# Part of the modulation weight loads issued by GpSimd instead of SyncE, in a four-layer DiT on one core

## The chip, the core and the metric

The kernel runs on one core of a Trainium2 chip. The core has a matrix engine (TensorE, PE in the profile, with its weight loads shown as PEld), a vector engine (VectorE, DVE), a scalar engine (ScalarE, ACT), a general engine (GpSimd, POOL) and a small engine that here does nothing but issue transfers (SyncE, SP). Each engine works through its own list of instructions in order; semaphores tell one engine that another, or a transfer, is done. The metric is device time in microseconds (us) of one execution, lower is better.

## The reference, cut to what matters

Four layers work on `x` (256 tokens of 2048 channels) and a context `ctx` of the same size, in fp32: layers 0 and 3 mix with a Fourier transform, layer 1 is attention with a window and the context, layer 2 is a conformer convolution. Every layer begins and ends with a modulation, and its weights are what this change is about:

```python
def ada_modulation(cond, w, b):
    m = jax.nn.silu(cond) @ w + b
    return jnp.split(m, 3, axis=-1)
...
    for i in range(DEPTH):
        ...
        shift, scale, gate = ada_modulation(c, ada_w[i], ada_b[i])
        h = rms_norm(x, norm_g[i]) * (1.0 + scale[:, None, :]) + shift[:, None, :]
        shift_c, scale_c, gate_c = ada_modulation(c_ctx, ada_w[i], ada_b[i])
        hc = rms_norm(ctx, norm_g[i]) * (1.0 + scale_c) + shift_c
        ...
        x = x + gate[:, None, :] * o
        if with_ctx:
            ctx = ctx + gate_c * oc
    return rms_norm(x, final_g)
```

`ada_w[i]` is 2048 x 6144 in fp32, 50 MB for each layer. It multiplies only two vectors (`c` and `c_ctx`), so almost all its cost is bringing it in.

## The kernel before, in words

**Matrix products.** Weights are loaded in pieces of 128 x 1024 (`raw`, issued on SP at L153, L155 and L157). ScalarE rounds each piece to a high half (`whi`, L181), and VectorE, in layer 2 partly GpSimd, takes the rest as a low half (`wlo`, L182). PE multiplies three times, high by high, low by high, high by low (L194 to L196 with the weights standing, L214 to L216 with the tokens standing).

**Modulation.** The 12 thirds of modulation weights are numbered (l, s): layer l, and s = 0 for shift, 1 for scale, 2 for gate. Shift and scale of layer 0 are computed by `ada_tiles` (L221) at the start. All others go through two objects of the class `Stream`: `ada_a` has (0,2), (1,0) and (1,1) and multiplies on PE (L271); `ada_v` has (1,2), (2,0), (2,1), (2,2), (3,0), (3,1), (3,2) and accumulates on DVE (L282 for the first piece of a third, L284 for the others), apart from a part of layer 2 in which it, too, uses PE. A third has 16 steps, and each step loads two tiles `aw` of 128 x 1024 (512 KB) in `Stream.get`, L331: 320 loads in all. The tiles come from one ring of four buffers (AWB = 4, tag "aw"), which both streams share, and two tiles of `ada_tiles` as well (L226). So a load can be issued only when the tile four places before it has been used up.

When a third on DVE is complete, its sum `adacc` is folded by PE (L298), copied (L301), transposed by small matmuls (L303), and becomes a part of `modc` (L309, L313). `adacc` has one buffer (L277): the next third cannot begin before that fold.

**Order.** The code calls `pump`, `step` and `until` of the streams between pieces of the matrix products (`plan` sets how many steps fall on how many pieces). That order is only a wish. The framework's scheduler then places every instruction in its engine's list by its own model of when operands and queues become free. An instruction's place in an engine's list can therefore change when a transfer is put on another queue, though no code near it was touched.

**Stages** in the profile of before: the start, with x, ctx and the first tiles of layer 0, until about 70 us; layer 0's z and shift/scale together to about 250 us, the rest of layer 0 to 700; keys and values of layer 1 (`do_kv`, L906) to 830; its attention (`do_q` L882, `do_attn` L939) to 1024; its z product and output product (L1003, L1023) to 1182; then layers 2 and 3.

**What shares SP with the loads.** Besides L331, SP issues all raw weights, the loads of x and ctx (L620), and the tiles of `ada_tiles` (L231). ScalarE issues a few small loads at the start. GpSimd issues none; it fills a few small tiles at the start (L112 and others) and first works again at about 1174 us, with the low halves of layer 2.

Names for the steps below: `cT` is ctx transposed (L642), `hh`/`hl` the halves of layer 0's normalised input (L449, L450), `accz`, `accq`, `acco` the accumulators of the products for z, queries and output, `pT` and `v` the transposed probabilities and the values of attention, `po` its output (L970), `nmx` its row maxima (L958, L959).

Of the kernel before, what the change touches and what calls it, by code (L numbers as in the profile page):

```python
# [19 lines left out]
P = 128  # L20
D = 2048
# [47 lines left out]
def dit_kernel(ctx: ExitStack, tc: tile.TileContext, x, c, ctxt, c_ctx, norm_g, ada_w, ada_b,  # L69
               four_w_in, four_w_out, attn_w_in, attn_sink, attn_w_out, conv_w_in, conv_dw_w,  # L70
               conv_dw_b, conv_ln_g, conv_ln_b, conv_w_out, final_g, dft, rope, maskc, out):
    nc = tc.nc
# [16 lines left out]
    def nm(s):  # L89
        uid[0] += 1  # L90
        return f"{s}_{uid[0]}"
# [226 lines left out]
    class Stream:  # L318
# [7 lines left out]
        def get(self, l, s, kt):  # L326
            aw = []
            for h in range(2):
                t = wp.tile([P, D // 2], F32, tag="aw", bufs=AWB, name=nm("aw"))
                c0 = s * D + h * (D // 2)  # L330
                nc.sync.dma_start(t[:], ada_w[l, kt * P:(kt + 1) * P, c0:c0 + D // 2])  # L331
                aw.append(t)
            return aw

# [668 lines left out]
    for g in range(4):  # L1003
        accs = [accA("accz") for _ in range(2)]
        gemm_T(outs2(accs), lambda kt: w_piece(w_rows(wi, kt, 2560 + g * 512)), rhsx, range(0, KT, 2), pump1)
        for i in range(2):
# [4 lines left out]
            t = hp.tile([P, 2, 512], F32R, tag=f"hc{2 * g + i}", name=nm("yh1"))  # L1011
# [106 lines left out]
    for cg in range(8):  # L1118
# [8 lines left out]
        for ci in range(2):  # L1127
            kt = 2 * cg + ci
# [207 lines left out]
```

## Time and profile before

| | before |
|---|---|
| median of 3 runs | 1928.31 us (1928.18 to 1931.59) |
| profiled execution | 1930.65 us |
| its span, first to last instruction | 1928.5 us |
| instructions in the span | 30124 |
| mean granted PE clock | 0.986 of full speed |
| bytes moved | 433.63 MB, mean 225 GB/s |
| loads `aw` (L231 and L331) | 376 issues of 512 KB on SP, median 5.4 us to landing |

The profile is one execution recorded by the hardware. Times in it are on its own scale: 2.15 us lie outside the span, and this execution was 2.34 us longer than the median. Busy time tells how full an engine is; the chain that ended last tells what released what, followed back from the end. An engine's idle time matters only where PE, or whatever sets the end of a stage, waits for it.

### The profile page before, as it was taken

Reading aid. Unit: us, or ns where it says so; the run is one execution under the profiler, and the core shown is the slowest. Engines: PE = TensorE matmul, PEld = TensorE weight load, DVE = VectorE, ACT = ScalarE, POOL = GpSimd, SP = SyncE. Lnnn points to the kernel's source line nnn. Section 1 sums busy time; section 2 is a strip of 40 time slices with the busy share of each in tenths; the row PEclk is TensorE's granted clock in tenths of the full one; section 3 lists DMA queues with packets and bytes.
Section 4 is the critical chain, followed back from the end, with each engine's and each line's share of the span. In section 5 each row is a group of like instructions: output and inputs, shape, how many; then the busy total and the mean of one; then the engine's idle time right before and its main releaser. Section 6 shows DMA issues by size and latency. Waiting matters only on the chain.

```text
span 1928.5 us, 30124 instructions
## 1 busy us (share of the span) xinstructions
PE 1852.9 (96%) x11143; PEld 1506.8 (78%) x11143; DVE 1441.8 (75%) x2719; ACT 892.7 (46%) x1606; POOL 228.0 (12%) x127
## 2 busy tenths in 40 slices
PE   6999999999999999999999999899998998999997
PEld 5566657777766787766689887899998887899886
DVE  4899944566654459977897796588899998897675
ACT  6333342224331236465555445444445656556553
POOL 0000000000000000000000002788880002000000
PEclk9999999999999999999999999999998998999999
DMA  8888878666677745831667695476765795876553
GB/s 257 282 297 301 300 245 271 206 232 207 233 269 265 272 151 161 275 120 55 206 208 251 227 320 197 159 232 212 234 230 175 245 322 169 290 273 176 163 175 131
DMA packets 247236, 433.63 MB, mean 225 GB/s; under 512 B 16214, under 2 KB 135734, under 8 KB 247090
## 3 DMA queue, kind: packets, MB, share of 16 engines
q1 hardware_dynamic: 245664, 430.00, 67.5%
q10 hardware_dynamic: 1426, 1.73, 0.3%
q8 instruction: 87, 1.43, 0.3%
q14 instruction: 59, 0.48, 0.1%
HBM read 429.56 MB, written 2.10 MB: 224 GB/s over the span
## 4 chain that ended last, share of the span: by engine, by line
PE 78%; DVE 9%; DMA 6%; issue 3%; ACT 2%; POOL 0%; SPq 0%; DVEq 0%; ACTq 0%; POOLq 0%
PE acco L1040 8%; PE accz L194 6%; PE accz L195 6%; PE accz L196 6%; DMA aw<-in_ada_w_dram 5%; PE acco L1041 4%; PE accu L214 4%; PE accu L215 4%; PE accu L216 4%; PE pa L271 3%; PE accg L194 3%; PE accg L196 3%; PE accg L195 3%; PE acco L194 3%; DVE wlo L182 3%
## 5 line engine op out<-in xcount | busy, mean ns | idle before, releaser
L181 ACT CAST whi<-raw 128x512 fp32r<-128x512 f32 (+1 forms) x764 | 540.8, 758 | 693.0 <-PE accz L195 133.0
L182 DVE TENSOR_TENSOR wlo<-raw,whi 128x512 fp32r<-128x512 f32 x680 | 492.0, 770 | 202.4 <-ACT whi L181 197.7
L182 POOL TENSOR_TENSOR wlo<-raw,whi 128x1024 fp32r<-128x1024 f32 x84 | 203.8, 2434 | 1371.6 <-ACT whi L181 1370.6
L284 DVE SCALAR_TENSOR_TENSOR adacc<-aw,csil,adacc 128x1024 f32<-128x1024 f32 x188 | 243.9, 1302 | 85.7 <-DMA aw<-in_ada_w_dram 85.2
L1040 PE MATMUL acco<-yh,whi 128*128 128x512 f32 x768 | 270.4, 397 | 0.2 <-DVE xT L1048 0.2
L196 PE MATMUL accz<-hx,wlo 128*128 128x256 f32 x768 | 221.1, 289 | 12.1 <-DVE wlo L182 12.0
L195 PE MATMUL accz<-hx,whi 128*128 128x256 f32 x768 | 220.9, 288 | 3.6 <-DVE hx L450 3.6
L194 PE MATMUL accz<-hx,whi 128*128 128x256 f32 x768 | 220.9, 288 | 1.1 <-ACT hx L449 1.1
L1041 PE MATMUL acco<-yh,wlo 128*128 128x256 f32 x768 | 215.2, 280 | 1.2 <-DVE wlo L182 1.2
L1139 DVE SCALAR_TENSOR_TENSOR pv<-gp,dwT,pv 128x256 f32<-128x256 f32 x480 | 191.1, 482 | 24.8 <-ACT pv L1133 24.4
L1040 PEld LDWEIGHTS acco<-yh,whi 128*128 128x128 f32 x768 | 144.1, 188 | 34.6 <-ACT yh L479 0.8
L196 PEld LDWEIGHTS accz<-hx,wlo 128*128 128x128 f32 x768 | 150.1, 196 | 14.1 <-DVE wlo L182 13.1
L195 PEld LDWEIGHTS accz<-hx,whi 128*128 128x128 f32 x768 | 150.3, 196 | 5.4 <-DVE hx L450 4.2
L194 PEld LDWEIGHTS accz<-hx,whi 128*128 128x128 f32 x768 | 150.3, 196 | 3.0 <-ACT hx L449 1.8
L196 PE MATMUL accg<-hx,wlo 128*128 128x256 f32 x512 | 146.6, 286 | 2.8 <-POOL wlo L182 2.7
L194 PE MATMUL accg<-hx,whi 128*128 128x256 f32 x512 | 147.5, 289 | 1.1 <-ACT hx L449 1.1
L1041 PEld LDWEIGHTS acco<-yh,wlo 128*128 128x128 f32 x768 | 144.8, 189 | 2.2 <-DVE wlo L182 2.1
L195 PE MATMUL accg<-hx,whi 128*128 128x256 f32 x512 | 146.4, 286 | 0.0
L194 PEld LDWEIGHTS accg<-hx,whi 128*128 128x128 f32 x512 | 99.6, 195 | 8.5 <-issue 6.9
L194 PE MATMUL acco<-yh,whi 128*128 128x512 f32 (+1 forms) x272 | 105.0, 387 | 0.0
L196 PEld LDWEIGHTS accg<-hx,wlo 128*128 128x128 f32 x512 | 99.6, 195 | 4.3 <-POOL wlo L182 3.4
L195 PE MATMUL acco<-yl,whi 128*128 128x512 f32 (+1 forms) x272 | 102.8, 378 | 0.0
(261 smaller groups left out, 3579.9 us busy)
## 6 DMA issues: line engine op xcount, KB each, us to landing
aw<-in_ada_w_dram SPq DMA_DIRECT2D x376, 512.0 KB, 5.4
raw<-in_four_w_in_dram SPq DMA_DIRECT2D x126, 512.0 KB, 4.6
raw<-in_attn_w_in_dram SPq DMA_DIRECT2D x72, 512.0 KB, 3.6
raw<-in_conv_w_in_dram SPq DMA_DIRECT2D x128, 256.0 KB, 2.9
raw<-in_four_w_out_dram SPq DMA_DIRECT2D x32, 512.0 KB, 6.7
raw<-in_attn_w_out_dram SPq DMA_DIRECT2D x64, 256.0 KB, 4.3
raw<-in_conv_w_in_dram SPq DMA_DIRECT2D x32, 512.0 KB, 4.4
raw<-in_conv_w_out_dram SPq DMA_DIRECT2D x64, 256.0 KB, 4.6
```

Of the source, the lines that this page charges most:

```text
L181: nc.scalar.copy(hv[:, c], iv[:, c])
L182: eng.tensor_sub(lv[:, c], iv[:, c], hv[:, c].bitcast(F32))
L194: mm(o, a, hh, start=st, stop=False, skip_group_check=True)
L195: mm(o, a, hl, start=False, stop=False, skip_group_check=True)
L196: mm(o, b, hh, start=False, stop=kt + k == span[1] - 1, skip_group_check=True)
L214: mm(acc[:], hh, whi[:, k, :], start=st, stop=False)
L215: mm(acc[:], hh, wlo[:, k, :], start=False, stop=False)
L216: mm(acc[:], hl, whi[:, k, :], start=False, stop=kt + k == KT - 1)
L284: ins = nc.vector.scalar_tensor_tensor(acc[:, cs], aw[i][:], cc, acc[:, cs], op0=ALU.mult, op1=ALU.add)
L1040: mm(o[:], whi[:, k, cs], rhs(kt), start=kt == 0, stop=False, skip_group_check=True)
L1041: mm(o[:, :256], wlo[:, k, cs], rhs(kt)[:, :256], start=False, stop=kt == KT - 1, skip_group_check=True)
L1139: nc.vector.scalar_tensor_tensor(pv[:, :256], gt[:, t:t + 256], dwT[:, kt, t:t + 1], pv[:, :256], op0=ALU.mult, op1=ALU.add)
```

## The change

One line: which engine issues the load in `Stream.get`.

```diff
             for h in range(2):
                 t = wp.tile([P, D // 2], F32, tag="aw", bufs=AWB, name=nm("aw"))
                 c0 = s * D + h * (D // 2)
-                nc.sync.dma_start(t[:], ada_w[l, kt * P:(kt + 1) * P, c0:c0 + D // 2])
+                (nc.sync if l == 3 or s == 2 and l == 2 else nc.gpsimd).dma_start(t[:], ada_w[l, kt * P:(kt + 1) * P, c0:c0 + D // 2])
                 aw.append(t)
             return aw
```

GpSimd now issues the six thirds (0,2), (1,0), (1,1), (1,2), (2,0) and (2,1): 6 x 16 x 2 = 192 loads. SP keeps (2,2) and layer 3, 128 loads. The condition covers layer 0's gate as well. Bytes, tiles and buffers are the same. SP's list becomes 192 rows shorter and GpSimd's 192 longer, and the scheduler's order changes on the other engines.

The first place is the start. GpSimd's list begins, after its small fills, with loads of the third (1,2):

```order
L112 MEMSET one_78 128x1
L331 DMA aw_2097<-in_ada_w_dram 128x1024
L331 DMA aw_2099<-in_ada_w_dram 128x1024
L331 DMA aw_2104<-in_ada_w_dram 128x1024
L331 DMA aw_2106<-in_ada_w_dram 128x1024
L331 DMA aw_2110<-in_ada_w_dram 128x1024
L331 DMA aw_2112<-in_ada_w_dram 128x1024
```

aw_2104 and aw_2106 take the buffers that `ada_tiles` used and wait for PE's last use of them; each later load waits for the accumulate four places before. In SP's list of before, aw_2097 stood behind the loads of L231.

DVE's list at that place, before, where transposed ctx (cT) is copied out:

```order
L450 SCALAR_TENSOR_TENSOR hl_325<-tmp_365,modc_87,hh_324 128x256
L182 TENSOR_TENSOR wlo_303<-raw_300,whi_302 128x2x128x2
L642 COPY cT_116<-pxt_449 128x512
L642 COPY cT_118<-pxt_463 128x512
L642 COPY cT_120<-pxt_477 128x512
L648 TENSOR_REDUCE ssc<-ssn 128x2
```

and now, with accumulates into adacc_2101, the sum of (1,2):

```order
L450 SCALAR_TENSOR_TENSOR hl_325<-tmp_365,modc_87,hh_324 128x256
L182 TENSOR_TENSOR wlo_303<-raw_300,whi_302 128x2x128x2
L284 SCALAR_TENSOR_TENSOR adacc_2101<-aw_2104,csil,adacc_2101 128x1024
L284 SCALAR_TENSOR_TENSOR adacc_2101<-aw_2106,csil,adacc_2101 128x1024
L284 SCALAR_TENSOR_TENSOR adacc_2101<-aw_2110,csil,adacc_2101 128x1024
L284 SCALAR_TENSOR_TENSOR adacc_2101<-aw_2112,csil,adacc_2101 128x1024
L284 SCALAR_TENSOR_TENSOR adacc_2101<-aw_2116,csil,adacc_2101 128x1024
L642 COPY cT_116<-pxt_449 128x512
L284 SCALAR_TENSOR_TENSOR adacc_2101<-aw_2118,csil,adacc_2101 128x1024
L642 COPY cT_118<-pxt_463 128x512
L642 COPY cT_120<-pxt_477 128x512
L648 TENSOR_REDUCE ssc<-ssn 128x2
```

Six accumulates have moved up among the copies. Further ones follow: aw_2130, aw_2134, aw_2136 and aw_2140 stand ahead of the low half wlo_667, where none of them stood before. By place in the list, aw_2097 goes from row 49 to 29, aw_2110 from 123 to 41, aw_2140 from 201 to 69.

The second place is the end of layer 1, after attention: DVE's list around the first accumulates of (2,2) (adacc_9165, loads on SP in both). Before, they stood inside attention:

```order
L990 TENSOR_TENSOR on_7522<-po_7582,rb_7607 128x256
L182 TENSOR_TENSOR wlo_8231<-raw_8228,whi_8230 128x512
L282 TENSOR_SCALAR adacc_9165<-aw_9161,csil 128x1024
L958 TENSOR_REDUCE nmx_7836<-s_7841 128x1
L282 TENSOR_SCALAR adacc_9165<-aw_9163,csil 128x1024
L959 TENSOR_TENSOR nmx_7836<-nmx_7836,nsink 128x1
L958 TENSOR_REDUCE nmx_7838<-s_7855 128x1
L284 SCALAR_TENSOR_TENSOR adacc_9165<-aw_9264,csil,adacc_9165 128x1024
```

Now they stand among the low halves of z's weights, with the fold's last steps (modc_89) between them:

```order
L182 TENSOR_TENSOR wlo_9171<-raw_9168,whi_9170 128x512 x2
L282 TENSOR_SCALAR adacc_9165<-aw_9161,csil 128x1024
L182 TENSOR_TENSOR wlo_9203<-raw_9200,whi_9202 128x512 x2
L309 TENSOR_TENSOR modc_89<-pa_9148,adabT 128x16
L282 TENSOR_SCALAR adacc_9165<-aw_9163,csil 128x1024
L313 SCALAR_TENSOR_TENSOR modc_89<-modc_89,ngT 128x16
L284 SCALAR_TENSOR_TENSOR adacc_9165<-aw_9264,csil,adacc_9165 128x1024
L182 TENSOR_TENSOR wlo_9235<-raw_9232,whi_9234 128x512 x2
```

The start of (2,2) went from row 1001 to row 1183 of DVE's list. On PE, the fold of (2,1) that frees adacc (L298, pa_9148) was split in one matmul at row 3326, among `accq`, and three at row 3686, just ahead of a `po` of attention; it is now at rows 3944 and 4310, among the `accz` matmuls of z, the last of them behind attention's last `po` (row 4183). From attention's end to layer 2, DVE's list now holds all 32 accumulates of (2,2) and the first 18 of (3,0), where 23 accumulates lay before.

In the stage of keys and values, three accumulates (aw_8360, aw_8362 and aw_8860) now stand ahead of rope (L850, L856) and of the low halves wlo_7039 and wlo_7059.

## The prediction

> **What bounds the kernel now.** I read the shares of busy time first, then the chain that ended last, then a table of busy time by stage.
>
> ```profile
> PE 1852.9 (96%) x11143; PEld 1506.8 (78%) x11143; DVE 1441.8 (75%) x2719; ACT 892.7 (46%) x1606; POOL 228.0 (12%) x127
> ...
> PE 78%; DVE 9%; DMA 6%; issue 3%; ACT 2%; POOL 0%; SPq 0%; DVEq 0%; ACTq 0%; POOLq 0%
> ```
>
> TensorE is busy for 96% of the span, and 78% of the chain lies on it. The chain also runs 9% over VectorE (DVE) and 6% over transfers, so I looked at such an excursion before believing in it. Around 600 us the chain leaves PE and comes back:
>
> ```profile
> 584.03 4.03 DMA aw<-in_ada_w_dram
> 588.09 1.29 DVE adacc L284
> ...
> 601.85 8.18 DMA aw<-in_ada_w_dram
> 610.07 1.03 PE pa L271 x4
> ```
>
> The excursion covers 26 us, but PE worked through it; the PE timeline shows what the wait at its end was worth, 0.72 us:
>
> ```profile
> 610.07 1.03 PE L271 MATMUL pa<-aw,csil 128*2 128x512 f32 x4 [0.72 <-DMA aw<-in_ada_w_dram]
> ```
>
> So a modulation load on the chain is not yet time to be won. By stage (columns: window, length, busy PE, PEld, DVE, ACT, POOL, clock, DMA share, GB/s):
>
> ```profile
> 5.00:30.00 25.00, 15.99 (x89) 10.73 (x90) 12.36 (x33) 15.48 (x35) 0.00 (x0) 0.93 1.08 327
> 30.00:40.00 10.00, 9.23 (x84) 7.61 (x82) 3.27 (x7) 9.75 (x25) 0.00 (x0) 1.00 0.31 90
> 40.00:70.00 30.00, 27.78 (x167) 17.23 (x165) 19.86 (x38) 12.66 (x21) 0.00 (x0) 1.00 0.91 299
> 70.00:250.00 180.00, 175.99 (x849) 118.89 (x850) 166.95 (x250) 73.46 (x91) 0.00 (x0) 1.00 0.83 285
> 250.00:700.00 450.00, 447.86 (x2230) 327.32 (x2230) 238.28 (x405) 135.48 (x252) 0.00 (x0) 1.00 0.73 247
> 700.00:830.00 130.00, 124.56 (x617) 100.42 (x615) 108.81 (x213) 62.75 (x140) 0.00 (x0) 1.00 0.61 197
> 830.00:1024.00 194.00, 194.00 (x1222) 141.39 (x1221) 163.84 (x410) 118.68 (x285) 0.00 (x0) 1.00 0.46 144
> 1024.00:1182.00 158.00, 156.54 (x1061) 141.54 (x1061) 118.28 (x189) 75.75 (x136) 4.58 (x2) 1.00 0.79 259
> ```
>
> From 250 to 1182 us PE idles 2.1 + 5.4 + 0.0 + 1.5 = 9.0 us of 932. That is the most that any better feeding can win there. What can be lost has no such bound: DVE stands at 93% in 70 to 250 us and at 75% in 1024 to 1182, and the transfers at 299 to 327 GB/s in three stages.
>
> **What leaves SP.** 192 of the 320 loads of L331 change queue.
>
> ```profile
> L331 SPq DMA_DIRECT2D aw<-in_ada_w_dram x320: 327/341/1258, 38.3 to 1720.0; - x160
> ...
> DMA to landing us min/median/max: 3.6/5.5/8.3
> ```
>
> SP is relieved of 192 x 0.341 = 65 us of issue work and of a part of its waits for buffers:
>
> ```profile
> SPq L331 <- DVE adacc L284: 101.8, 87, 5.2
> ...
> SPq L331 <- PE pa L271: 101.2, 40, 5.6
> ...
> SPq L331 <- DMA aw<-in_ada_w_dram: 83.8, 30, 5.8
> ```
>
> Those 286.8 us held the weight loads behind them, but PE's 9.0 us of idle time say that the weights were there anyhow. Loads that SP now brings sooner are worth what PE still waited for. Of that, only its waits for modulation rows are directly the change's own:
>
> ```profile
> PE pa L271 <- DMA aw<-in_ada_w_dram: 1.6, 4, 0.7
> ```
>
> I take **-1.6 us**, with 0 and half of 9.0 (-4.5) as ends.
>
> **The start.** The trace of before has no load on GpSimd's queue. The nearest rows are the same loads on SP: 5.5 us over the whole run, and in the first 60 us
>
> ```profile
> aw<-in_ada_w_dram SPq DMA_DIRECT2D x10, 512.0 KB, 6.3
> ```
>
> with 8.3 us the longest of all. GpSimd has nothing else to do at the start, so its queue runs ahead where SP's had first to come past layer 0's own loads (first L331 issue 38.3 us). The order shows the effect: only 1 step of the group (1,2) stood ahead of the first weight splits; now 7 accumulates stand among the transposes of ctx and 14 ahead of wlo_667. DVE works in order, so its ctx copies and weight splits wait for transfers that did not concern them. The first four loads that take over the ring's buffers wait for PE's release of layer 0's tiles:
>
> ```profile
> 21.08 0.61 PE L235 MATMUL pa<-aw,csil 128*2 128x256 f32 x8
> ```
>
> (the row before it starts at 20.17). Take 20.8 us as the issue of aw_2104. Then each round of four is one issue (0.341), a landing and an accumulate (1.29 in the chain above), because the buffer that a load takes is freed by the accumulate four before it; three such rounds lie before aw_2140, the last accumulate ahead of wlo_667. The rows that this must be held against are
>
> ```profile
> 34.49 0.69 DVE L642 COPY cT<-pxt 128x512 f32<-128x512 f32 x1 [6.18 <-PE pxt L638]
> ...
> 50.61 1.10 DVE L182 TENSOR_TENSOR wlo<-raw,whi 128x512 fp32r<-128x512 f32 x1 [1.78 <-ACT whi L181]
> ```
>
> Three rounds with landings of 5.5, 6.3 and 8.3 us take 21.4, 23.8 and 29.8 us. To these come the last round's other three accumulates (3.9) and some 4.8 us of DVE's own rows between (four copies like the one at 34.49, 2.8 in all, and about 2 us of smaller ones). The split then comes at 50.9, 53.3 or 59.3 in place of 50.61: +0.3, +2.7 or +8.7. That is DVE's side. The transfers have another: 14 loads x 0.524 MB = 7.3 MB come in before some 61 us that came later, and what was free at 327 GB/s is (327 - 90) x 10 us = 2.4 MB from 30 to 40 us and (327 - 299) x 30 us = 0.8 MB after it. The other 4.1 MB push x's, ctx's and layer 0's loads back by up to 12.6 us. PE is at 93% of 30 to 70 us, so a push is not absorbed. Ends +0.3 and +12.6; I take **+8**, near the 8.3 us landing, since these loads meet the fullest transfers of the kernel (327 GB/s).
>
> What DVE has done early it need not do later, but from 70 to 250 us PE is busy 175.99 of 180 us, so nothing is won there: **0**.
>
> **Keys and values of layer 1.** Three accumulates (3 x 1.29 = 3.9 us) of (2,1) now stand ahead of rope and of two weight splits. PE's only wait there is
>
> ```profile
> PE pkt L930 <- ACT kd L924: 2.0, 1, 2.0
> ```
>
> Loads that come sooner could take these 2.0 us away; the accumulates ahead could lengthen it by 3.9. I take **+1**.
>
> **The tail of layer 1.** The fold of (2,1) moves from 909 us to behind the last of attention, because its loads are consumed later in the new order. adacc has one buffer, so (2,2), whose loads stay on SP, cannot begin before it. DVE's accumulates in the tail were
>
> ```profile
> 1024.00:1182.00 158.00, 1.06 (x8) 0.16 (x8) 28.17 (x23) 1.00 0.79 259
> ```
>
> and 50 stand there now: 27 more at 28.17/23 = 1.22 us are 33.1 us. DVE goes from 118.3 to 151.4 of 158 us, 96%. The 27 bring 14.2 MB; four of these loads can wait in the ring before (2.1 MB), so 259 GB/s x 158 us = 40.9 MB becomes 53.0 MB. The best stretch in this stage moved
>
> ```profile
> 1120.00:1160.00 40.00, 40.00 (x233) 34.92 (x232) 34.84 (x59) 18.56 (x35) 0.00 (x0) 1.00 0.96 327
> ```
>
> and with its neighbours (321 over 1100 to 1160) some 324 GB/s; 53.0 MB take 163.6 us, 5.6 more than there are. What hides the accumulates is DVE's idle time of 39.7 us; most of it is waiting for ScalarE in order:
>
> ```profile
> L182 DVE TENSOR_TENSOR wlo<-raw,whi 128x512 fp32r<-128x512 f32 x104 | 67.2, 686 | 28.6 <-ACT whi L181 27.6 <-issue 0.9
> ```
>
> If none of those 27.6 us can be used, 151.4 + 27.6 = 179.0 us, +21. If the accumulates spread evenly, 0. I take **+5.6**. Later stages keep their queue and their rows move by a few places: 0.
>
> **Sum.** -1.6 + 8 + 0 + 1 + 5.6 = +13.0 on the profiled execution's 1930.65 us (span 1928.5 and 2.15 around it) gives 1943.7. That execution is 2.34 us above the median of the runs, 1928.31; so 1941.3, and I say **1941 us**.
>
> **Rivals.**
> *The queue does not matter.* PE's waits for modulation rows are 1.6 us, 27 accumulates fit into 39.7 us of idle DVE, and ctx is transposed while DVE idles 6.18 us. Then -1.6 and some 2 at the start cancel: 1929 us. For it: PE at 99% over 250 to 1182 us. Against it: the start, where DVE's order changes beside the fullest transfers. The Trainium skill, "DMA: Bandwidth & Descriptors", section "Issuing engines are not separate DMA queues", says the same in general: whatever engine issues, the transfers share the same 16 DMA engines, and a second issuer saves only issuing time. By that alone the sum would be this rival's; no trace here has yet shown it.
>
> *Faster, through SP.* With 65 us of issues and part of 286.8 us of waits gone, raw weights are fetched a buffer's turn earlier, ScalarE's halves come sooner, and half of PE's 9.0 us between 250 and 1182 us goes, -4.5. It decides if loads at the start land within 5.5 us, so that the split stays at 50.9. 1928.31 - 4.5 - 0.3 is about 1923.5 us.
>
> *Much slower, DVE in order.* Both upper ends: rounds of 9.9 us at the start (8.3 + 0.34 + 1.28; +8.7 to +12.6) and the tail's +21, with -1.6: about 1930.65 + 12.6 + 21 + 1 - 1.6 - 2.34 = 1961 us. It decides if the splits of z's weights each wait for a modulation load in front of them. Against it: L284 waited for transfers only 2.2 us in all in that stage.
>
> The same page's "Specifications" give about 1 us to the first byte from GpSimd and 0.6 from SP; by these, as an estimate, three rounds would cost 1.2 us more. No row of before bears on it.
>
> **How the numbers follow.** Forecast 0.56; no matter 0.22; faster 0.13; much slower 0.09. All lower ends together (+0.3, 0, -2.0, -4.5) reach 1922, but they are the third rival; I go from 1925, half-way into it, to 1957, short of the last. Left out are 0.09, some 0.07 of the fast case and a little of the forecast's own upper end. A measurement can tell 0.2% (3.9 us) from no change: below 1924.5 is faster, above 1932.2 slower. Faster 0.13, same 0.22, slower 0.65 (forecast and last rival).
>
> **What would show it.** Start: the fourth ctx copy (38.52 us) and the split at 50.61 come later by 2 to 9 us, with adacc among them, and PE's first z matmuls with them. If the split is within 0.5 us, the start is wrong. Tail: fold of (2,1) behind attention, some 50 accumulates between attention's end and layer 2, the stage longer than 158 us by about 5. If PE still fills 99% of it, the tail is wrong. Prediction wrong as a whole: if the loads on GpSimd's queue land much later than 8.3 us, or if PE's busy time itself changes through its clock (0.986 now).

## The result, and the profile after

| | before | changed |
|---|---|---|
| median | 1929.25 us (4 runs, 1928.18 to 1931.59) | 1963.28 us (4 runs, 1960.34 to 1970.41) |
| ratio to before | | 1.0174, 95% interval 1.0156 to 1.0192 |
| span of the profiled execution | 1928.5 us | 1958.5 us |
| granted PE clock | 0.986 | 0.982 |

The changed kernel is 34 us slower by the medians, 30 by the profiled executions (that of the changed kernel was the fastest of its four). To see where the 30 us arise, I followed PE through the program: the last matmul of the first product of layer 0 (L697), the first `acco` matmul of layer 1's output product (L1040), the first `accg` matmul of layer 2 (L194). The groups of PE instructions say when the first and the last of each starts. Before:

```profile
L697 PE MATMUL accz<-hh,wlo x32: 279/283/415, 27.7 to 49.2; 128*128 128x256 f32 x32
...
L1040 PE MATMUL acco<-yh,whi x768: 389/395/496, 1087.5 to 1914.9; 128*128 128x512 f32 x192
...
L194 PE MATMUL accg<-hx,whi x512: 278/283/582, 1187.6 to 1396.1; 128*128 128x256 f32 x171
```

Changed:

```profile
L697 PE MATMUL accz<-hh,wlo x32: 279/283/415, 29.8 to 62.1; 128*128 128x256 f32 x32
...
L1040 PE MATMUL acco<-yh,whi x768: 387/395/632, 1102.7 to 1944.7; 128*128 128x512 f32 x192
...
L194 PE MATMUL accg<-hx,whi x512: 278/283/580, 1218.6 to 1425.0; 128*128 128x256 f32 x171
```

The start costs 62.1 - 49.2 = 12.9 us. It stays at that, with 2 us more by 1102.7. From the first `acco` to the first `accg` it now takes 115.9 us in place of 100.1: another 15.8. After that nothing is added: the last `acco` is 29.8 us later. So most of the loss sits in the two places that the prediction named, and both are larger than it said. I call the stretch between the two groups **the tail** below.

The stages at the start in the changed kernel (columns as in the prediction's table) show the transfers full without a gap and PE short of work, where before 30 to 40 us had been nearly free:

```profile
5.00:30.00 25.00, 13.87 (x79) 8.55 (x80) 12.95 (x35) 14.71 (x33) 2.28 (x4) 0.96 1.07 361
30.00:40.00 10.00, 10.00 (x72) 9.15 (x74) 5.43 (x6) 7.60 (x18) 2.11 (x4) 0.75 1.08 370
40.00:70.00 30.00, 21.23 (x134) 15.46 (x127) 22.41 (x35) 12.53 (x25) 4.75 (x9) 0.83 0.97 327
```

In the DVE timeline the ctx copy that stood at 34.49 us comes at 40.95, behind an accumulate that waited for its load, as the order had suggested:

```profile
39.74 1.29 DVE L284 SCALAR_TENSOR_TENSOR adacc<-aw,csil,adacc 128x1024 f32<-128x1024 f32 x1 [4.49 <-DMA aw<-in_ada_w_dram]
40.95 0.68 DVE L642 COPY cT<-pxt 128x512 f32<-128x512 f32 x1
```

This looks like the cause. The experiments show that it is not, and two views of this trace already speak against it. PE's waits from 5 to 75 us, the first row before and the other two changed, put 1.5 us on the copies and 6.9 on layer 0's own tiles:

```profile
PE pa L235 <- DMA aw<-in_ada_w_dram: 2.5, 3, 0.9
```

```profile
PE pa L235 <- DMA aw<-in_ada_w_dram: 6.9, 3, 3.8
PE pxt L638 <- DVE cT L642: 1.5, 2, 1.3
```

And the first weight split behind the copies, at 47.71 us before, comes at 60.60, after DVE had stood idle for it, waiting for ScalarE's high half and not for an accumulate:

```profile
60.60 1.13 DVE L182 TENSOR_TENSOR wlo<-raw,whi 128x512 fp32r<-128x512 f32 x1 [2.39 <-ACT whi L181]
```

The DMA issues of the first 60 us, before and then changed, show something else: layer 0's own tiles of 256 KB, which PE needs for its first modulation, land after 9.8 us in place of 5.9.

```profile
DMA packets 15544, 15.34 MB, mean 256 GB/s; under 512 B 815, under 2 KB 13108, under 8 KB 15540
...
aw<-in_ada_w_dram SPq DMA_DIRECT2D x16, 256.0 KB, 5.9
```

```profile
DMA packets 15643, 20.60 MB, mean 343 GB/s; under 512 B 970, under 2 KB 11562, under 8 KB 15639
...
aw<-in_ada_w_dram POOLq DMA_DIRECT2D x17, 512.0 KB, 7.0
aw<-in_ada_w_dram SPq DMA_DIRECT2D x16, 256.0 KB, 9.8
```

At the end of layer 1 the two windows are attention and what follows it to layer 2:

```profile
850.00:1037.00 187.00, 187.00 (x1171) 135.50 (x1169) 129.51 (x360) 108.77 (x266) 0.00 (x0) 1.00 0.24 73
1037.00:1213.00 176.00, 163.62 (x1062) 143.27 (x1063) 148.04 (x216) 76.57 (x139) 5.08 (x4) 0.99 0.90 305
```

The same second window for the accumulates alone:

```profile
1037.00:1213.00 176.00, 2.12 (x14) 0.31 (x14) 61.29 (x50) 0.99 0.90 305
```

In attention the transfers run at 73 GB/s, for no modulation load is left to bring: the last one on GpSimd's queue was issued at 820.4 us, and (2,2) waits for the fold. Then all 50 accumulates of the order fall into the last window, which moves 305 GB/s x 176 us = 53.7 MB. PE waits there for low halves that DVE makes late:

```profile
PE acco L1041 <- DVE wlo L182: 7.0, 6, 3.2
PE acco L1040 <- ACT whi L181: 2.1, 2, 1.4
PE pa L271 <- DMA aw<-in_ada_w_dram: 1.8, 1, 1.8
```

Before, the first of these rows was 1.2 us.

### The profile page after: what moved, and what is told of

The parts are those of the page before. It is cut to its first block, busy times and chain, and to the rows that moved or that the text cites. A ratio compares the mean times of both kernels' runs of the same rounds, so it can differ in the third digit from the quotient of the medians.

```text
span 1958.5 us, 30172 instructions
## 1 busy us (share of the span) xinstructions
PE 1862.3 (95%) x11143; PEld 1510.9 (77%) x11143; DVE 1442.3 (74%) x2719; ACT 887.7 (45%) x1602; POOL 331.3 (17%) x319
## 4 chain that ended last, share of the span: by engine, by line
PE 47%; issue 23%; DMA 17%; DVE 8%; POOL 2%; ACT 1%; SPq 1%; POOLq 0%; DVEq 0%; ACTq 0%
DMA aw<-in_ada_w_dram 14%; PE acco L1040 7%; PE acco L1041 3%; PE accz L196 3%; PE accz L194 3%; PE accz L195 3%; PE accg L194 3%; PE accg L196 3%; PE accg L195 3%; DVE wlo L182 3%; PE po L970 2%; PE ppt L964 1%; DVE adacc L284 1%; DMA raw<-in_attn_w_out_dram 1%; POOL aw L331 1%
## 5 line engine op out<-in xcount | busy, mean ns | idle before, releaser
L1040 PE MATMUL acco<-yh,whi 128*128 128x512 f32 x768 | 271.6, 399 | 3.5 <-ACT whi L181 2.1
L196 PE MATMUL accz<-hx,wlo 128*128 128x256 f32 x768 | 221.7, 289 | 11.2 <-DVE wlo L182 10.7
L331 POOL DMA_DIRECT2D aw<-in_ada_w_dram x192 | 101.7, 532 | 717.7 <-DVE adacc L284 347.7
L194 PE MATMUL accz<-hx,whi 128*128 128x256 f32 x768 | 221.3, 289 | 1.1 <-ACT hx L449 1.1
L1040 PEld LDWEIGHTS acco<-yh,whi 128*128 128x128 f32 x768 | 143.8, 189 | 38.3 <-ACT whi L181 3.9
L194 PEld LDWEIGHTS accz<-hx,whi 128*128 128x128 f32 x768 | 149.8, 195 | 3.9 <-ACT hx L449 1.8
L194 PE MATMUL accg<-hx,whi 128*128 128x256 f32 x512 | 146.8, 287 | 1.6 <-ACT hx L449 1.1
L726 DVE TENSOR_TENSOR y<-accz,y 128x512 f32<-128x512 f32 x128 | 85.0, 689 | 30.0 <-PE accz L196 29.8
L194 PEld LDWEIGHTS accg<-hx,whi 128*128 128x128 f32 x512 | 98.9, 193 | 9.4 <-issue 6.9
L194 PE MATMUL acco<-yh,whi 128*128 128x512 f32 (+1 forms) x272 | 105.2, 387 | 0.3 <-DVE cT L787 0.3
```

The source lines that it names most:

```text
L194: mm(o, a, hh, start=st, stop=False, skip_group_check=True)
L196: mm(o, b, hh, start=False, stop=kt + k == span[1] - 1, skip_group_check=True)
L331: (nc.sync if l == 3 or s == 2 and l == 2 else nc.gpsimd).dma_start(t[:], ada_w[l, kt * P:(kt + 1) * P, c0:c0 + D // 2])
L726: nc.vector.tensor_add(y, accs[ci][:], y)
L1040: mm(o[:], whi[:, k, cs], rhs(kt), start=kt == 0, stop=False, skip_group_check=True)
```

## The experiments

All times are compared with the kernel before, measured on the same chip beside them. Its median was 1930.31 us beside e1 to e4, 1930.92 beside e5 to e8, 1931.97 beside e9 to e11 and 1931.88 beside e12 and e13. Its single times spread over 1925.8 to 1939.1 us, so I rest on the ratios and, for single places, on the profile.

| run | median, us | ratio (95% interval) | L697 ends at | tail |
|---|---|---|---|---|
| before (first profile) | - | 1 | 49.2 | 100.1 |
| changed | 1963.28 | 1.0174 (1.0156 to 1.0192) | 62.1 | 115.9 |
| e1, (1,2) alone | 1941.63 | 1.0052 (1.0035 to 1.0070) | 60.5 | 99.5 |
| e2, (2,0) and (2,1) alone | 1956.65 | 1.0135 (1.0108 to 1.0162) | 49.6 | 119.4 |
| e3, PE's stream alone | 1932.85 | 1.0010 (0.9995 to 1.0024) | 49.9 | 100.6 |
| e4, changed, fold early | 1944.65 | 1.0068 (1.0047 to 1.0088) | 59.8 | 100.5 |
| e5, e1 held behind | 1934.94 | 1.0017 (1.0001 to 1.0032) | 51.1 | 99.9 |
| e6, e1 with half the bytes | 1936.84 | 1.0027 (1.0012 to 1.0043) | 54.4 | 100.9 |
| e12, e1 with narrow accumulates | 1948.14 | 1.0082 (1.0053 to 1.0111) | 63.9 | 100.6 |
| e7, e2 with half the bytes | 1946.84 | 1.0082 (1.0045 to 1.0118) | 50.1 | 108.2 |
| e8, e2 with narrow accumulates | 1950.15 | 1.0089 (1.0059 to 1.0120) | 49.4 | 107.3 |
| e13, e2 with both cuts | 1946.65 | 1.0075 (1.0052 to 1.0098) | 49.7 | 103.3 |
| e11, e2 with the tail's loads on GpSimd | 1958.27 | 1.0139 (1.0117 to 1.0162) | 49.2 | 114.0 |
| e9, changed, both put right | 1944.05 | 1.0069 (1.0052 to 1.0086) | 50.8 | 103.2 |
| e10, before, fold early | 1940.84 | 1.0048 (1.0033 to 1.0063) | 49.6 | 100.2 |

The last two columns are single profiled executions, in us. "L697 ends" is the start of the last matmul of that group; the expectations call it the last L695 matmul.

### Which thirds cost the time

e1 moves only (1,2):

```diff
-(nc.sync if l == 3 or s == 2 and l == 2 else nc.gpsimd)
+(nc.gpsimd if (l, s) == (1, 2) else nc.sync)
```

> Only the third (1,2), 32 of the 192 loads, goes to GpSimd. Theory (two places): the +30 us of the profiled execution is some +13 at the start, all of it from this third, whose loads run ahead of layer 0's own, and some +16 in the tail of layer 1, from (2,0) and (2,1). So this run is 13 us above before, about 1942 us: the last L695 matmul at about 62 us in place of 49.2, and the tail as before (layer 2's first accg some 100 us behind the first acco of layer 1's output). Rival (the queue itself is dear, each load costs the same wherever it stands): 32/192 of the loss, +6 us, about 1935. Rival (transfers only collide in the tail): 1929.

e2 moves only (2,0) and (2,1):

```diff
-(nc.sync if l == 3 or s == 2 and l == 2 else nc.gpsimd)
+(nc.gpsimd if l == 2 and s < 2 else nc.sync)
```

> Only (2,0) and (2,1), 64 of the 192 loads, go to GpSimd. Theory (two places): the start is as before (last L695 at 49 us), the fold of (2,1) stands behind attention, (2,2) is crowded into the tail, +16 us: about 1945 us. Rival (dear queue): 64/192 of the loss, +11, about 1940, spread over layers 0 and 1 and not in the tail. Rival (tail only by what the start displaced): 1929.

e3 moves only the stream on PE:

```diff
-(nc.sync if l == 3 or s == 2 and l == 2 else nc.gpsimd)
+(nc.gpsimd if (l, s) in ((0, 2), (1, 0), (1, 1)) else nc.sync)
```

> Only (0,2), (1,0) and (1,1), the 96 loads of the stream on PE, go to GpSimd; DVE's order is that of before. Theory (two places): neither place is touched, so 1929 us within 4. Rival (dear queue): half of the loss, +15 us, about 1944. Rival (SP's relief is worth something): up to 4.5 us faster, 1925.

The 96 loads of e3, half of the 192 moved, cost nothing that can be measured. The 32 of e1 alone make 11.3 of the start's 12.9 us, and the tail is as before. The 64 of e2 alone make the tail's loss and more (19.3 us, the changed kernel 15.8), and the start is as before. The queue as such is not dear: the rival that charges every load alike is out. e2 is nearly 12 us above its expectation of 1945. Some 3.4 of them are in the tail (119.4 where the theory had 116). The profile of e2 also loses 5.1 us in layer 0's output product (from the last matmul of the product before it, `accu`, to the last `acco`: 221.7 us in place of 216.6), and e3, whose profile is the longest of its ten executions, loses 5.0 there (221.6). The changed kernel has 218.3. No run was made for that.

e4 is the changed kernel with the fold put early:

```diff
         do_attn(g, qT)
+        if g == 0:
+            ada_v.until(2, 1)
         if g < 3:
```

> The changed kernel with one call more: after the first head group of attention the third (2,1) is closed, so that its fold stands early in PE's list and (2,2) is accumulated inside attention, where the transfers of the changed kernel moved only 73 GB/s. Theory (two places): the tail's +16 us goes and the start's +13 stays, about 1942 to 1947 us; the stage from the first acco of layer 1's output to the first accg of layer 2 takes about 100 us again in place of 116. Rival (loads on GpSimd's queue land too late for the tail, wherever the fold stands): 1963. Rival (attention has no room on DVE): the loss moves into attention, po's last matmul later by 10 us or more, total near 1960.

(2,2) is then accumulated inside attention, and the tail is back at 100.5 us. It is the fold's place, not the landing of loads, that crowded the tail. The time is within the expectation, though the way from the keys and values to the first `acco` is 4.4 us longer (294.7 us in place of 290.3); see e10 below for what an early fold costs.

### What the start's loss is made of

e5 orders both first accumulates of (1,2) behind the first L726 add, with the means the kernel has for it (`ada_v.behind`):

```diff
-                nc.vector.tensor_add(y, accs[ci][:], y)
+                ins = nc.vector.tensor_add(y, accs[ci][:], y)
+                if j == 1 and cg == 0 and ci == 0:
+                    ada_v.behind = ins
...
-                        ada_v.behind = None
+                        ada_v.behind = None if i or l != 1 else ada_v.behind
```

> As the run with only the third (1,2) on GpSimd, but both first accumulates of (1,2) are ordered on DVE behind the first L726 add, so that DVE's list at the start has no accumulate among the ctx copies and the ring lets only four loads run ahead. Theory (DVE's order and the early loads it lets through make the start's loss): the last L695 matmul comes at 51 us or so, 2 us behind before for the first two loads that lie beside x's, in place of 60.3; the time is 1929 to 1933 us. Rival (loads on GpSimd's queue slow those of SP at the start in any order): the last L695 stays near 60, time 1941.

The start's loss falls from 11.3 to 1.9 us; the median, 1934.94 us, is a little above the theory's 1933. But this takes two things away at once: the accumulates among the ctx copies, and the loads that their buffers let through. e6 cuts the bytes and keeps the DVE work and its order:

```diff
-                nc.sync.dma_start(t[:], ada_w[l, kt * P:(kt + 1) * P, c0:c0 + D // 2])
+                wl = D // 4 if (l, s) == (1, 2) and kt < 12 else D // 2
+                (nc.gpsimd if (l, s) == (1, 2) else nc.sync).dma_start(t[:, :wl], ada_w[l, kt * P:(kt + 1) * P, c0:c0 + wl])
...
+                    if (l, s) == (1, 2) and kt < 12:
+                        av = av.rearrange("p (a b) -> p a b", a=2)
+                        src = aw[i][:, :w // 2].unsqueeze(1).to_broadcast([P, 2, w // 2])
...
```

> As the run with only (1,2) on GpSimd, but its first 24 loads bring 512 of 1024 columns, and the accumulate reads these twice: the same DVE work in the same order with half the bytes (the output is not that of the reference). If the transfers make the start's loss: 3.7 MB less at some 350 GB/s is 10 us, the last L695 at 50 to 53 us in place of 60.3. If DVE's order makes it (each accumulate waits for a landing of mostly fixed length): 57 to 60. If both share it: 54 to 57.

Half the bytes gives back 6.1 of the 11.3 us: the case in which both share it. With 18.10 MB in the first 60 us, e6 still brings 2.8 MB more than before. e12 cuts the DVE work and keeps the bytes:

```diff
-                    cs = slice(w * i, w * i + w)
+                    cs = slice(w * i, w * i + (64 if (l, s) == (1, 2) and 0 < kt < 12 else w))
...
```

> As the run with only (1,2) on GpSimd, with all bytes and the same order on DVE, but the accumulates of steps 1 to 11 take 64 of 1024 columns, about 1.2 us of DVE less each (the output is not that of the reference). Half the bytes took the last L695 from 60.5 to 54.4 us. If the rest is DVE's own work: 54 to 56 here too. If DVE only waits for landings, and these are long because the transfers are full: 58 us or more, since the buffers come free sooner and as many bytes come in.

This decides it. With DVE's part nearly gone the start is not faster but slower, 63.9 us. The DVE timeline of e12 (where L642 is L643) shows two ctx copies at 37.91 and 39.44 us, earlier than in the changed kernel, and the next one waiting for PE:

```profile
39.44 0.68 DVE L643 COPY cT<-pxt 128x512 f32<-128x512 f32 x1
...
44.04 0.69 DVE L643 COPY cT<-pxt 128x512 f32<-128x512 f32 x1 [2.97 <-PE pxt L639]
```

PE in turn waits for layer 0's tiles:

```profile
PE pa L235 <- DMA aw<-in_ada_w_dram: 8.9, 3, 3.8
```

against 3.3 us in e5, where the last L697 matmul comes at 51.1, and 6.9 in the changed kernel. PE's wait for the ctx copies, 2.0 us in e1, is no longer among its waits in e12. So the mechanism is the transfers. Loads that layer 1 needs run ahead and share the way with loads that layer 0 needs now. The median landing of layer 0's sixteen 256 KB tiles and the start's end are both later where more bytes come in during the first 60 us; among the last three rows, all above 20 MB, the bytes no longer give the order:

| run | bytes in the first 60 us, MB | landing of the 256 KB tiles, us | L697 ends at, us |
|---|---|---|---|
| before | 15.34 | 5.9 | 49.2 |
| e5 | 16.79 | 6.9 | 51.1 |
| e6 | 18.10 | 7.0 | 54.4 |
| e1 | 20.80 | 9.6 | 60.5 |
| changed | 20.60 | 9.8 | 62.1 |
| e12 | 20.24 | 9.8 | 63.9 |

DVE's accumulates among the ctx copies are hardly a cost by themselves: the most that PE waited for the copies is 1.5 us in the changed kernel and 2.0 in e1. Their part is that they free the ring's buffers and so let the next load go.

### What the tail's loss is made of

e7 and e8 make the same two cuts for the 50 loads and 46 accumulates of the tail, on top of e2.

> As the run with (2,0) and (2,1) on GpSimd, but the 50 loads of (2,2) and the start of (3,0) bring half of their columns, read twice by the accumulate: the same DVE work, 13.1 MB less (the output is not that of the reference). If the transfers bound the tail: from the first acco of layer 1's output to the first accg of layer 2 it takes about 100 us again in place of 119, time about 1937. If DVE bounds it (148 of 176 us busy, in order): 115 us or more, time about 1955.

> As the run with (2,0) and (2,1) on GpSimd, with all bytes, but 46 of the accumulates of (2,2) and (3,0) in the tail take only 64 of 1024 columns: about 1.1 us of DVE less each, 50 us in all (the output is not that of the reference). If DVE's work bounds the tail: about 100 us in place of 119. If the transfers bound it: 112 us or more. If both must be there for the loss, each of the two runs (half the bytes, narrow accumulates) recovers most of it.

Of 19.3 us, half the bytes gives back 11.2 and narrow accumulates 12.1. Both runs lie between their two expectations, and each recovers most of the loss, as e8's third case has it. So neither the transfers nor DVE alone bounds the tail. The windows over the stage show why the one cut does not bring it down to 100. e7 first, then e8:

```profile
1028.00:1196.00 168.00, 160.76 (x1073) 144.00 (x1071) 152.62 (x217) 77.10 (x139) 9.04 (x7) 0.99 0.79 253
```

```profile
1032.00:1199.00 167.00, 160.37 (x1063) 141.80 (x1062) 105.83 (x216) 77.15 (x139) 5.71 (x6) 1.00 0.93 320
```

With half the bytes DVE is still busy for 152.6 of 168 us; with narrow accumulates the transfers run at 320 GB/s. e13 makes both cuts:

> As the run with (2,0) and (2,1) on GpSimd, with half the bytes for the 50 tail loads and 46 of their accumulates 64 columns wide, both cuts at once (the output is not that of the reference). Alone, the cuts brought the tail from 119.4 to 108.2 and 107.3 us, before has 100.1. If bytes and DVE's work are the whole cause: 100 to 102 us. If a third cause (raw loads behind modulation loads in SP's list, or the late fold itself) has a part: 104 us or more.

The tail is 103.3 us: the two together are 16.1 of the 19.3 us. They overlap (11.2 + 12.1 is 23.3). I explain that by the ring of four buffers: a load waits for an accumulate, the accumulate stands in DVE's list behind and ahead of low halves, and the low halves' raw weights share the way with the load. No run changed the ring, so this is not shown. The 3.2 us left lie between the two expectations, so a small third cause stays possible. The time of e13 is no better than that of e7 because its profile also loses 5.7 us in layer 0's output product and 4.3 between the keys and values and the first `acco`.

e11 asks whether SP's list has a part, by sending the tail's loads to GpSimd as well:

```diff
-(nc.gpsimd if l == 2 and s < 2 else nc.sync)
+(nc.gpsimd if l == 2 or (l, s) == (3, 0) and kt < 9 else nc.sync)
```

> As the run with (2,0) and (2,1) on GpSimd, but (2,2) and the first nine steps of (3,0) go there too, so that in the tail no modulation load stands in SP's list between the raw weights. Bytes and DVE work in the tail are those of that run. If SP's order (a raw load behind a modulation load that waits for the ring) makes a good part of the 19 us: the tail in 105 to 110 us. If only bytes and DVE's order count: 115 us or more.

The tail is 114.0 us, between the two expectations, 5.4 us shorter than in e2. But from the keys and values to the first `acco` e11 takes 297.7 us, e2 293.2, so 4.5 of the 5.4 us have only moved, and the time does not gain by it. A large part of SP's order in the tail's loss is not seen.

### Both put right, and the fold alone

e9 is the changed kernel with e5's order at the start and e4's early fold; e10 is the kernel before with the early fold.

> The changed kernel, all six thirds on GpSimd, with both places put right: the first accumulates of (1,2) behind the first L726 add, and (2,1) closed after the first head group of attention. Theory (start and tail are the whole loss): the last L695 at 51 us, the first accg of layer 2 some 100 us behind the first acco of layer 1's output, time 1930 to 1935 us, at most 0.3% above before. Rival (a third loss sits in the queue itself): 1940 or more. Rival (SP's relief shows once the order is right): below 1926.

> The kernel before, all loads on SP, with (2,1) closed after the first head group of attention, so that (2,2) is accumulated inside attention. PE was busy 156.54 of 158 us in the tail of before, so theory says no change: 1930 us within 3. Rival (before, too, lost time in the tail that an early fold wins): the tail below 98 us and 1927 or less. Rival (attention is crowded by the accumulates): po's last matmul later by 5 us, 1935.

Both miss. e9 is at 1944.05 us although its start costs 1.6 us and its tail 3.1. That is the time of its rival, a loss in the queue itself, but e10 has no load on GpSimd and, with nothing changed but the fold's place, is 0.48% slower than before. The early fold is not free. The rival of e10 had the right stage and the wrong sign: `po`'s last matmul comes 5.2 us earlier (1019.6 us, before 1024.8), not later. What is longer is the stage's beginning: from the end of keys and values to the first `acco` e10 takes 298.1 us in place of 290.3. The first `po` matmul comes 41.5 us after the last of the keys and values in place of 33.6, so the loss lies where (2,1) ends and attention begins. PE's windows there:

```profile
797.00:800.00 3.00, 2.49 (x11) 1.00 0.99 376
800.00:805.00 5.00, 3.54 (x11) 0.68 0.90 329
805.00:815.00 10.00, 10.00 (x50) 0.99 0.70 237
815.00:820.00 5.00, 2.79 (x14) 0.89 0.99 363
820.00:825.00 5.00, 5.00 (x26) 0.77 0.43 125
```

PE has two gaps, while 329 to 376 GB/s come in, and after each its clock is down. That loads and accumulates of (2,2) collide with the rest there, as in the tail, is read from these windows and was not tried by itself. e9 has 3.7 us of this (294.0), and 2.9 in layer 0's output product. No version that was run beats the kernel before; e3 stands beside it.

## Why the prediction was wrong

**The whole.** Forecast was +13 on the profiled execution, measured +30; 1963 us lies above the range's upper end of 1957. The direction and both places were right. Two terms of the sum were too small.

**The start, +8 forecast, +12.9 measured.** The step that failed is the choice of the mechanism that sizes it. The prediction had two sides, rounds of DVE (+0.3 to +8.7) and the transfers (4.1 MB too many, +12.6), and went near DVE's upper end. e12 shows that the loss stays when most of DVE's work for these accumulates is gone, and e6 that it shrinks with the bytes. The transfers' side was put down as an upper end when it was the estimate. That it came within 0.3 us is partly luck: 3.6 of the 12.9 us are a slower clock of PE (below), which the sum does not contain.

**The tail, +5.6 forecast, +15.8 measured.** What moves was right: 50 accumulates stand there (61.29 us of DVE, forecast 28.2 + 33.1 = 61.3), and 53.7 MB were moved (forecast 53.0). The step that failed is the overlap: the sum charged the transfers' 5.6 us and hid the added accumulates in DVE's idle time, at nothing, with +21 as an end that need not be reached. The runs show that both cost. With DVE's work cut (e8) the transfers reach 320 GB/s, close to the 324 of the sum, and the tail is still 7.2 us above before. With the bytes halved (e7) it is 8.1 above, with both cut (e13) 3.2, with neither (e2) 19.3. So the transfers' term was near by itself, DVE's was not nothing, and the two together cost more than each by itself: above e13's 3.2 they are 4.0, 4.9 and, together, 16.1. The 305 GB/s of the changed kernel's tail are what the two make of each other, not a limit of the transfers.

**Keys and values, +1.** From the last `acco` of layer 0 to the last matmul of keys and values it took 74.1 us against 74.6: nothing, within its range.

**SP's relief, -1.6.** Nothing of it is to be seen. e3 takes 96 loads from SP, touches neither of the two places, and is at 1.0010 (0.9995 to 1.0024); half of the 1.6 us would not stand out there.

**The rivals.** "The queue does not matter" holds for the queue alone, as e3 shows, and for 96 of the 192 loads. The Trainium skill ("DMA: Bandwidth & Descriptors", section "Issuing engines are not separate DMA queues") says that transfers of all issuers share the same 16 engines, and the trace agrees: with 5.3 MB more in the first 60 us, SP's own tiles land 3.9 us later. What it concludes, that another issuer only saves issuing time, does not follow for a program in which the issuer's list also decides when a load may go. "Much slower", 1961 us, came nearest in its number. It was given 0.09, as if both upper ends would have to fall together by chance. Both losses are of one kind, modulation loads that meet a stage whose transfers are full, so a sum that prices such a meeting too low is likely to be low in both; but e1 and e2 show that each arises without the other. Its mechanism, DVE in order, is not what the start shows, and its tail of +21 is too large, so the nearness is in part luck.

## What to carry to other kernels

These are lessons of one kernel. A queue that has nothing else to do runs ahead, as far as its buffers let it: here the first load of L331 is issued at 1.5 us in place of 38.3. Before a load is moved there, ask what it will then overtake, and take as a first size what comes in too early, divided by the rate of the fullest stage. Where a change lets work slide into a stage in which two resources are both well filled (here DVE at 84% and the transfers at 90%), do not choose one of the two bounds and hide the other behind it.

## What was not expected of the hardware

**A pause of PE is paid twice.** PE's windows from 40 to 65 us in the changed kernel (busy PE, granted clock, DMA share, GB/s):

```profile
40.00:45.00 5.00, 2.59 (x24) 1.00 1.11 351
45.00:50.00 5.00, 1.24 (x10) 0.86 1.05 370
50.00:55.00 5.00, 2.40 (x14) 0.50 1.04 368
55.00:60.00 5.00, 5.00 (x30) 0.62 1.03 337
60.00:65.00 5.00, 5.00 (x35) 1.00 0.62 199
```

From 40 to 50 us PE is idle for 6.2 us. The clock then falls to 0.50, and the first 5 us of full work run at 0.62; before, the clock stayed at 1.00 through the same windows. The whole stretch from 5 us to the end of layer 0's first product, before and then changed (all columns, as in the prediction's table):

```profile
5.00:49.50 44.50, 33.92 (x243) 25.26 (x247) 19.53 (x49) 31.10 (x71) 0.00 (x0) 0.96 0.88 270
```

```profile
5.00:62.40 57.40, 37.51 (x240) 28.62 (x240) 33.19 (x62) 31.39 (x71) 8.09 (x15) 0.85 1.05 356
```

PE idles 10.6 us before and 19.9 now, and is busy for 33.9 and 37.5. So of the start's 12.9 us, 9.3 are idle time and 3.6 are the same product taking longer at a mean clock of 0.85 in place of 0.96. The windows of e10 above show lower clocks too (0.68 and 0.77).

The Trainium skill ("TensorE: Matmul & The Clock Gate", section "Part 1: The HAM clock gate") states this: after an idle window of about 3.4 us the clock is halved until PE has been busy for as long. The trace agrees in the 0.50, which follows a wait of 3.8 us, but it also shows 0.51 from 30 to 35 us, after single waits of at most 1.75 us with PE busy for 2.16 of the 5 us before; an unbroken idle window is not needed here. The prediction left the clock out of its sum and named it only as a sign of being wrong. Here it made the gaps dearer than their length.

**Issuing from GpSimd.** One load of 512 KB takes 527 ns to issue there in the median (987 the longest), where SP took 341 before. The loads of L331 land after 5.7 us in the median of the changed kernel, 5.5 before. In e3 this made no difference to the time.

**What stays open.** Kernels in which one stream's loads are on SP and the other's on GpSimd (e2, e3, e7, e8, e11, e13) take 219 to 222 us for layer 0's output product, those with both on SP there 216 to 217, those with both on GpSimd 217 to 219.5 (e4, changed, e9). These are single profiles and it was not tried by itself. Open too are the 3.2 us that the tail keeps in e13, and the 2.3 us that the changed kernel loses between the start and the first `acco` of layer 1's output.
